# The second layer's modulation in a two-layer diffusion trunk: the context's gate and FFN entries are no longer computed

## The chip, the cores and the metric

The kernel runs on one core of one Trainium2 chip. The metric is the device time of one execution in microseconds (us). The kernel before was timed in three runs: 1600.06, 1601.11 and 1597.38, median 1600.06. All traces are of single profiled executions, and times in them count from the first instruction of the span.

## The reference, cut to what matters

Two streams run through two layers: 512 latent tokens `x` and 256 context tokens `ctx`, each 1024 wide. Each layer makes six modulation vectors of 1024 entries for each stream from one weight matrix `ada_w[layer]` (1024 x 6144): shift, scale and gate of the attention (0, 1, 2), and shift, scale and gate of the FFN (3, 4, 5).

```python
for layer in range(DEPTH):                      # DEPTH = 2
    ctx_out = layer < DEPTH - 1
    mod_x = split(silu(c) @ ada_w[layer] + ada_b[layer], 6)
    mod_c = split(silu(c_ctx) @ ada_w[layer] + ada_b[layer], 6)
    h_x = modulate(rmsnorm(x, norm_g[layer, 0]), mod_x[0], mod_x[1])
    h_c = modulate(rmsnorm(ctx, norm_g[layer, 0]), mod_c[0], mod_c[1])
    o_x, o_c = mixer(...)                       # latents read latents and context
    x = x + mod_x[2] * o_x
    h_x = modulate(rmsnorm(x, norm_g[layer, 1]), mod_x[3], mod_x[4])
    x = x + mod_x[5] * swiglu(h_x, w1[layer], w3[layer], w2[layer])
    if ctx_out:
        ctx = ctx + mod_c[2] * o_c
        h_c = modulate(rmsnorm(ctx, norm_g[layer, 1]), mod_c[3], mod_c[4])
        ctx = ctx + mod_c[5] * swiglu(h_c, w1[layer], w3[layer], w2[layer])
return rmsnorm(x, final_g)
```

In the last layer (`ctx_out` false) the context is only read by the attention: `mod_c[2]` to `mod_c[5]` of that layer appear in nothing that is returned.

## The kernel before, in words

Activations lie transposed: 1024 features as 8 tiles of 128 partitions, tokens along the free side. Every matmul of full precision is done in three, with each operand split into a high and a low half (`hi`, `lo`, both fp32r): hi x hi, hi x lo, lo x hi. The tiles of weights are therefore called `wh` and `wl`. A weight tile is made from a raw load in one of two ways. `split` (L198, L199) copies the high half on ScalarE (ACT) and subtracts on VectorE (DVE). `split_by_dma` (L203 to L205) writes the negative rounded value on ACT (L203), lets a DMA issued by GpSimd (POOL) add the raw value to it (L204), and copies the high half on ACT (L205).

The program runs in stages. The first 460 us hold the first layer's attention, up to 980 us follows the first layer's FFN, to 1232 us the second layer's attention, and then the second FFN and the final norm.

The change is in the first FFN. Its hidden tiles are worked on in pairs p = 0 to 10, grouped as [0, 1], [2], [3, 4], [5, 6], [7, 8], [9, 10] (`supers0`). From pair 2 on, a pair's product with w1 or with w3 is made by `seven` (L1512 to L1551): seven half-size products instead of eight, 84 matmuls of 384 columns, whose sums are formed on DVE out of PSUM (tile `f`). After the w1 product comes the SiLU on ACT (L1620); after the w3 product DVE multiplies (L1627), ACT casts the high half of `g` (L1632) and DVE subtracts the low half (L1632). L1531 copies the first of the seven products out of PSUM on ACT. After a group's first w1 product the group before it goes through its down product with w2 (`down`, L1561 to L1563), whose results are added to the residuals on DVE (L1555). So PE's order is, for instance: pair 5 w1, down of [3, 4], pair 5 w3, pair 6 w1, pair 6 w3, pair 7 w1, down of [5, 6], pair 7 w3.

The weights for `seven` also need sums of quarters of the raw tiles, made on DVE (L534, L535, L538, L539); L538 writes over raw data that the DMA of L204 has to have read. `wh` and `wl` have three buffers each, so a split can begin only when PE is done with the product three steps before, and raw tiles have three buffers too.

The second layer's modulation is computed in the same stretch, on DVE, as rows. `ada1` lists 52 rows: 4 of the first layer, then 8 for each of the six entries of the second layer. For a row, SyncE (SP) loads 128 x 1024 of the transposed `ada_w` (512 KB, two buffers, L623). DVE then multiplies it with the silu of `c` (tile `tables`, L271) and once more with the silu of `c_ctx` (tile `csr`, L272), and an accumulator sums along the row, which gives 128 entries of the vector for each stream. After a vector's eighth row L274 adds the bias, and for the scales L259 forms `amod`. `rows(n, after)` places n rows behind a given instruction: one or two with each step of the down products and one with most products of `seven`. The first 20 rows are the first layer's last four and the second layer's shift and scale of the attention; the other 32 are the entries 2 to 5. After the last row the tiles `tables` and `csr` are used again: L1435 and L1436 load the rope tables into `tables` from POOL's queue.

The order of the first layer's start is written by hand. Behind that (`by_hand.close()`) a planner with its own timeline sets the order of each engine's queue, under the constraints that `tc.issue_after` gives; each queue then runs in that order.

Of the kernel before, what the change touches and what calls it, by code (L numbers as in the profile page):

```python
# [11 lines left out]
ALU = mybir.AluOpType  # L12
# [3 lines left out]
P = 128  # L16
D = 1024
KT = D // P
# [19 lines left out]
def tile_trunk(  # L38
# [27 lines left out]
    nc = tc.nc  # L66
# [35 lines left out]
    adab = const.tile([P, 2, 6, KT], F32, name="adab")  # L102
    ng = const.tile([P, 2, 2, KT], F32, name="ng")
# [5 lines left out]
    mod = [const.tile([P, 6, 2, KT], F32, name=f"mod{l}") for l in range(2)]  # L109
    amod = [const.tile([P, 2, 2, KT], F32, name=f"amod{l}") for l in range(2)]  # L110
# [130 lines left out]
    def ada_out(sb, psum, pieces):  # L241

        pt = psum()
        for hh in range(2):
            nc.tensor.transpose(pt[:, hh * P : (hh + 1) * P], sb[:, hh * P : (hh + 1) * P], ident)
        for hh in range(2):
            src = pt[:, hh * P : (hh + 1) * P].rearrange("p (j w) -> p w j", w=32)[:, 0:2, :]
            for j0, nj, l, s, k0 in pieces:
                dst = mod[l][:, s, :, k0 : k0 + 2 * nj].rearrange("p v (j h) -> p v j h", h=2)[:, :, :, hh]
                b = adab[:, l, s, k0 : k0 + 2 * nj].rearrange("p (j h) -> p h j", h=2)[:, hh : hh + 1, :]  # L250
                nc.vector.tensor_add(dst, src[:, :, j0 : j0 + nj], b.to_broadcast([P, 2, nj]))
        for j0, nj, l, s, k0 in pieces:
            ada_scale(l, s, slice(k0, k0 + 2 * nj))

    def ada_scale(l, s, ks):

        if s in (1, 4):
            nk = ks.stop - ks.start
            nc.vector.scalar_tensor_tensor(  # L259
                amod[l][:, s // 3, :, ks],  # L260
                mod[l][:, s, :, ks],
                1.0,
                ng[:, l, s // 3 : s // 3 + 1, ks].to_broadcast([P, 2, nk]),
                op0=ALU.add,
                op1=ALU.mult,
            )

    def ada_rows(l, s, k, cs, raw, junk):

        col = mod[l][:, s, :, k : k + 1]  # L270
        nc.vector.scalar_tensor_tensor(junk, raw, 1.0, cs[0], op0=ALU.mult, op1=ALU.mult, accum_out=col[:, 0])  # L271
        nc.vector.scalar_tensor_tensor(junk, raw, 1.0, cs[1], op0=ALU.mult, op1=ALU.mult, accum_out=col[:, 1])  # L272
        if k == KT - 1:
            nc.vector.tensor_add(mod[l][:, s], mod[l][:, s], adab[:, l, s : s + 1, :].to_broadcast([P, 2, KT]))  # L274
            ada_scale(l, s, slice(0, KT))


# [349 lines left out]
    with ExitStack() as st:  # L627
# [625 lines left out]
        def row_pieces(n):  # L1253

            def f(s_, k):
                if (s_, k) == (2, 0):
                    load_rows([tables, rbuf])
                junk = rp.tile([P, NX], F32, tag="ru", name="junk", bufs=1).bitcast(mybir.dt.bfloat16)
                raw = S.next()
                if s_ < 5:  # L1260
                    return ada_rows(0, s_, k, [tables, rbuf], raw, junk)

                with tc.issue_after(last_sum[0].ins):
                    ada_rows(0, s_, k, [tables, rbuf], raw, junk)

            out_ = []
            for _ in range(n):
                s_, k = rows.pop(0)
                S.add(ada_wT0[s_ - 2, k] if s_ < 5 else ada_wT[k], "ada")
                out_.append(lambda s_=s_, k=k: f(s_, k))  # L1270
            return out_
# [116 lines left out]
    with ExitStack() as st:  # L1388
# [13 lines left out]
        junk = fp.tile([P, 1024], mybir.dt.bfloat16, name="junk")  # L1402
# [22 lines left out]
        def rows(n, after):  # L1425

            for _ in range(n):
                if ada_raw:
                    with tc.issue_after(after.ins):
                        ada_rows(*ada1[len(ada1) - len(ada1_load) - len(ada_raw)], csr, ada_raw.pop(0), junk)  # L1430
                        ada_request(apool)
# [739 lines left out]
```

## Time and profile before

| what | value |
|---|---|
| timed runs, median of 3 | 1600.06 us |
| profiled execution | 1595.57 us |
| its span | 1593.8 us, granted TensorE clock 0.995 |
| PE busy | 1544.4 us (97%) |
| weight loads on PE (PEld) busy | 1380.3 us (87%) |
| DVE busy | 1246.6 us (78%) |
| ACT busy | 735.4 us (46%) |
| POOL busy | 261.4 us (16%) |
| the first FFN, 459.5 to 980 | PE 516.69 of 520.50 us, DVE 430.73 |
| rows of weights (L271, L272) from 470 on | 52 each, 63.4 us each on DVE |

In a row of a group the profile gives line, engine, operation, tiles out<-in, shape and count, then busy time in us and the mean ns of one, then the idle time before it and what ended that. In a row of the timeline stand the start, the duration, the engine and the line. In a row of waits: who waited, for whom, the us in total, how often, and the longest. PE means matmuls, whose ends are modelled, and PEld their weight loads, which overlap them.

### The profile page before, as it was taken

To read this page: it belongs to the slowest core of one execution; us is meant where nothing else is said; L and a number is where in the kernel's file an instruction comes from. 1 tells how busy PE (TensorE), PEld (TensorE's weight loads), DVE (VectorE), ACT (ScalarE), POOL (GpSimd) and SP (SyncE) were. 2 spreads that over 40 slices of the span, in tenths; PEclk is the share of its full clock that TensorE was granted. 3 is DMA by queue.
4 is the path that set the end of the run, shared out by engine and by line. 5 is a ranking of instruction groups with operands and counts; after the bars stand their busy time and mean duration, and the time that the engine had idled before them with its cause. 6 is when DMAs were issued, how large, how long until landed. Compare 5 with 4: busy or idle time off the path is not lost.

```text
span 1593.8 us, 25582 instructions
## 1 busy us (share of the span) xinstructions
PE 1544.4 (97%) x9902; PEld 1380.3 (87%) x9902; DVE 1246.6 (78%) x2137; ACT 735.4 (46%) x1278; POOL 261.4 (16%) x303
## 2 busy tenths in 40 slices
PE   8999999999999999999999999999999999999997
PEld 5798988877788999989999998886778899989896
DVE  4777798867698789879798867687776887869686
ACT  4546555445354423433324254456764543425354
POOL 1032223462010000000101001254331000000001
PEclk9999999999999999999999999999999999999998
DMA  9322254543236466476757651410002342322321
GB/s 355 110 61 82 77 167 136 180 132 100 69 114 172 109 182 171 133 199 172 216 167 191 179 148 66 118 55 27 28 28 77 109 146 80 130 70 93 119 80 54
DMA packets 68449, 195.28 MB, mean 123 GB/s; under 512 B 6772, under 2 KB 19220, under 8 KB 68328
## 3 DMA queue, kind: packets, MB, share of 16 engines
q1 hardware_dynamic: 58136, 159.95, 31.2%
q0 software_dynamic: 9184, 32.39, 9.5%
q8 instruction: 78, 1.28, 0.3%
q10 hardware_dynamic: 1008, 1.31, 0.2%
q14 instruction: 43, 0.35, 0.1%
HBM read 160.45 MB, written 4.86 MB: 104 GB/s over the span
## 4 chain that ended last, share of the span: by engine, by line
PE 61%; DVE 5%; DMA 2%; issue 1%; ACT 1%; POOL 0%; DVEq 0%; POOLq 0%; ACTq 0%; SPq 0%
PE f L1522 5%; PE f L1520 5%; PE f L1521 5%; PE f L1952 4%; PE f L1951 4%; PE f L1950 4%; PE f L1562 3%; PE f L1561 3%; PE f L1563 3%; PE f L210 3%; PE f L211 3%; PE f L209 3%; PE f L2003 2%; PE f L2004 2%; PE f L2005 2%; PE t L410 2%
## 5 line engine op out<-in xcount | busy, mean ns | idle before, releaser
L198 ACT ACTIVATE wh<-raw 128x1024 fp32r<-128x1024 f32 (+1 forms) x96 | 92.2, 977 | 233.5 <-DVE raw L539 101.5
L209 PE MATMUL lin<-hb,wh 128*128 128x512 f32 (+1 forms) x440 | 157.3, 358 | 4.2 <-ACT hb L1293 1.8
L210 PE MATMUL lin<-hb,wh 128*128 128x512 f32 (+1 forms) x440 | 154.7, 352 | 0.5 <-DVE hb L1294 0.5
L211 PE MATMUL lin<-hb,wl 128*128 128x512 f32 (+1 forms) x440 | 154.2, 350 | 0.0
L199 DVE TENSOR_TENSOR wl<-raw,wh 128x1024 fp32r<-128x1024 f32 (+1 forms) x96 | 107.0, 1120 | 37.1 <-ACT wh L198 35.0
L271 DVE SCALAR_TENSOR_TENSOR junk<-raw,tables 128x1024 bf16<-128x1024 f32 x80 | 98.7, 1234 | 21.0 <-DMA raw<-in_ada_wT_dram 20.5
L204 POOL DMA_DIRECT2D wl<-raw x39 | 34.0, 873 | 443.9 <-ACT wl L203 367.0
L1561 PE MATMUL f<-g,wh 128*128 128x512 f32 (+1 forms) x304 | 102.8, 339 | 0.4 <-DVE s L1550 0.4
L1562 PE MATMUL f<-g,wh 128*128 128x512 f32 (+1 forms) x304 | 102.8, 339 | 0.0
L1951 PE MATMUL f<-hb,wh 128*128 128x256 f32 x360 | 101.7, 283 | 0.0
L1950 PE MATMUL f<-hb,wh 128*128 128x256 f32 x360 | 101.4, 283 | 0.0
L1952 PE MATMUL f<-hb,wl 128*128 128x256 f32 x360 | 101.2, 283 | 0.0
L1563 PE MATMUL f<-g,wl 128*128 128x256 f32 (+1 forms) x304 | 100.6, 336 | 0.0
L209 PEld LDWEIGHTS lin<-hb,wh 128*128 128x128 f32 x440 | 83.2, 189 | 18.6 <-issue 2.7
L1520 PE MATMUL f<-hb,wh 128*128 128x384 f32 x288 | 96.2, 334 | 0.0
L1521 PE MATMUL f<-hb,wh 128*128 128x384 f32 x288 | 96.2, 334 | 0.0
L1522 PE MATMUL f<-hb,wl 128*128 128x384 f32 x288 | 96.2, 334 | 0.0
L210 PEld LDWEIGHTS lin<-hb,wh 128*128 128x128 f32 x440 | 83.4, 189 | 11.0 <-DVE hb L1294 0.7
L211 PEld LDWEIGHTS lin<-hb,wl 128*128 128x128 f32 x440 | 83.3, 189 | 10.5
L161 DVE TENSOR_TENSOR wl<-raw,wh 128x1024 fp32r<-128x1024 f32 x57 | 74.5, 1309 | 15.9 <-ACT wh L160 15.8
L160 ACT CAST wh<-raw 128x1024 fp32r<-128x1024 f32 x57 | 59.7, 1048 | 55.3 <-PE t L210 14.9
L338 POOL TENSOR_TENSOR ns_a<-ns_a,ns_s 128x256 f32<-128x256 f32 (+1 forms) x12 | 12.2, 1019 | 420.7 <-ACT ns_s L334 414.1
(435 smaller groups left out, 4864.0 us busy)
## 6 DMA issues: line engine op xcount, KB each, us to landing
raw<-in_w_dram SPq DMA_DIRECT2D x132, 512.0 KB, 3.8
raw<-in_ada_wT_dram SPq DMA_DIRECT2D x80, 512.0 KB, 4.0
wl<-raw POOLq DMA_DIRECT2D x39, 512.0 KB, 6.6
raw<-in_w_ab_dram SPq DMA_DIRECT2D x24, 512.0 KB, 3.9
raw<-in_ada_w_dram SPq DMA_DIRECT2D x12, 512.0 KB, 8.1
raw<-in_w_c_dram SPq DMA_DIRECT2D x12, 512.0 KB, 3.5
nb<-in_na_bias_dram POOLq DMA_DIRECT2D x16, 256.0 KB, 3.3
raw<-in_wo_ab_dram SPq DMA_DIRECT2D x8, 512.0 KB, 3.5
```

Source lines behind the costliest of these rows:

```text
L209: nc.tensor.matmul(ps, wh(k), xh(k), start=k == 0, stop=False)
L210: nc.tensor.matmul(ps, wh(k), xl(k), start=False, stop=False)
L211: end = nc.tensor.matmul(ps, wl(k), xh(k), start=False, stop=k == n - 1)
L1520: nc.tensor.matmul(ps, wh(k), b[:, 0, :], start=k == 0, stop=False)
L1521: nc.tensor.matmul(ps, wh(k), b[:, 1, :], start=False, stop=False)
L1522: nc.tensor.matmul(ps, wl(k), b[:, 0, :], start=False, stop=k == 3)
L1561: nc.tensor.matmul(ps, hi, g[:, 0, cols[v]], start=first, stop=False)
L1562: nc.tensor.matmul(ps, hi, g[:, 1, cols[v]], start=False, stop=False)
L1563: nc.tensor.matmul(ps, lo, g[:, 0, cols[v]], start=False, stop=last)
L1950: nc.tensor.matmul(ps, wh(k), b[:, 0, :], start=k == 0, stop=False)
L1951: nc.tensor.matmul(ps, wh(k), b[:, 1, :], start=False, stop=False)
L1952: nc.tensor.matmul(ps, wl(k), b[:, 0, :], start=False, stop=k == 3)
```

## The change

`sides(l, s)` says for how many streams an entry of a layer is computed: one, the latent, for the second layer's entries 2 to 5, and two elsewhere. `ada_rows` then issues one accumulating instruction a row and not two, and the bias addition and the `amod` of these entries cover 8 columns and not 16. All rows of weights are still loaded.

```diff
+    def sides(l, s):
+
+        return 1 if l and s > 1 else 2
+
     def ada_scale(l, s, ks):
 
         if s in (1, 4):
-            nk = ks.stop - ks.start
+            nk, nv = ks.stop - ks.start, sides(l, s)
             nc.vector.scalar_tensor_tensor(
-                amod[l][:, s // 3, :, ks],
-                mod[l][:, s, :, ks],
+                amod[l][:, s // 3, 0:nv, ks],
+                mod[l][:, s, 0:nv, ks],
                 1.0,
-                ng[:, l, s // 3 : s // 3 + 1, ks].to_broadcast([P, 2, nk]),
+                ng[:, l, s // 3 : s // 3 + 1, ks].to_broadcast([P, nv, nk]),
                 op0=ALU.add,
                 op1=ALU.mult,
             )
 
     def ada_rows(l, s, k, cs, raw, junk):
 
-        col = mod[l][:, s, :, k : k + 1]
-        nc.vector.scalar_tensor_tensor(junk, raw, 1.0, cs[0], op0=ALU.mult, op1=ALU.mult, accum_out=col[:, 0])
-        nc.vector.scalar_tensor_tensor(junk, raw, 1.0, cs[1], op0=ALU.mult, op1=ALU.mult, accum_out=col[:, 1])
+        col, n = mod[l][:, s, :, k : k + 1], sides(l, s)
+        for i in range(n):
+            nc.vector.scalar_tensor_tensor(junk, raw, 1.0, cs[i], op0=ALU.mult, op1=ALU.mult, accum_out=col[:, i])
         if k == KT - 1:
-            nc.vector.tensor_add(mod[l][:, s], mod[l][:, s], adab[:, l, s : s + 1, :].to_broadcast([P, 2, KT]))
+            nc.vector.tensor_add(mod[l][:, s, 0:n], mod[l][:, s, 0:n], adab[:, l, s : s + 1, :].to_broadcast([P, n, KT]))
             ada_scale(l, s, slice(0, KT))
```

Because a planner sets the order, other instructions move as well, from the down product of [3, 4] to the end of the first FFN; outside it every queue keeps its order. In the changed kernel the lines from 259 on have numbers higher by 4, and L271 and L272 are one line, L276.

The first place is DVE's queue in the down product of [3, 4], before the change. `junk` with `tables` is the latent's sum of a row, `junk` with `csr` the context's, `res` with `f` and `mod` a residual addition, and `raw` with `res` a sum of weight quarters.

```order
L271 SCALAR_TENSOR_TENSOR junk,mod_111<-raw,tables 128x1024
L272 SCALAR_TENSOR_TENSOR junk,mod_111<-raw,csr_4798 128x1024
L1555 SCALAR_TENSOR_TENSOR res<-f,mod_110,res 128x512
L1555 SCALAR_TENSOR_TENSOR res<-f,mod_110,res 128x256
L1555 SCALAR_TENSOR_TENSOR res<-f,mod_110,res 128x512
L1555 SCALAR_TENSOR_TENSOR res<-f,mod_110,res 128x256
L271 SCALAR_TENSOR_TENSOR junk,mod_111<-raw,tables 128x1024
L272 SCALAR_TENSOR_TENSOR junk,mod_111<-raw,csr_4798 128x1024
L271 SCALAR_TENSOR_TENSOR junk,mod_111<-raw,tables 128x1024
L538 TENSOR_TENSOR raw<-res,raw 128x512
L272 SCALAR_TENSOR_TENSOR junk,mod_111<-raw,csr_4798 128x1024
L539 TENSOR_TENSOR raw<-raw 128x512
```

The same place after the change:

```order
L276 SCALAR_TENSOR_TENSOR junk,mod_111<-raw,tables 128x1024
L539 TENSOR_TENSOR raw<-raw 128x512
L199 TENSOR_TENSOR wl<-res,wh 128x512
L1559 SCALAR_TENSOR_TENSOR res<-f,mod_110,res 128x512
L1559 SCALAR_TENSOR_TENSOR res<-f,mod_110,res 128x256
L1559 SCALAR_TENSOR_TENSOR res<-f,mod_110,res 128x512
L1559 SCALAR_TENSOR_TENSOR res<-f,mod_110,res 128x256
L276 SCALAR_TENSOR_TENSOR junk,mod_111<-raw,tables 128x1024 x2
L542 TENSOR_TENSOR raw<-res,raw 128x512
L1559 SCALAR_TENSOR_TENSOR res<-f,mod_110,res 128x512
L1559 SCALAR_TENSOR_TENSOR res<-f,mod_110,res 128x256
L543 TENSOR_TENSOR raw<-raw 128x512
```

The sums with `csr` are gone, a row with `tables` has moved behind the four residual additions, and the sums of quarters (L538, now L542) have fewer rows ahead of them.

The second place is ACT's queue from pair 6's w1 to pair 6's w3, before the change; `wl<-raw` (L203) is the first step of `split_by_dma`, `g<-q` the cast behind a w3 product and `q<-q` the SiLU.

```order
L205 CAST wh<-raw 128x1024
L203 ACTIVATE wl<-raw 128x1024
L1632 CAST g<-q 128x1536
L1531 COPY s<-f 128x384
L198 ACTIVATE wh<-res 128x512
L198 ACTIVATE wh<-raw 128x1024 x2
L205 CAST wh<-raw 128x1024
L203 ACTIVATE wl<-raw 128x1024
L1620 ACTIVATE q<-q 128x1536
L1531 COPY s<-f 128x384
```

After the change:

```order
L205 CAST wh<-raw 128x1024
L1636 CAST g<-q 128x1536
L1535 COPY s<-f 128x384
L203 ACTIVATE wl<-raw 128x1024
L198 ACTIVATE wh<-res 128x512
L198 ACTIVATE wh<-raw 128x1024 x2
L1624 ACTIVATE q<-q 128x1536
L1535 COPY s<-f 128x384
L205 CAST wh<-raw 128x1024
L203 ACTIVATE wl<-raw 128x1024
```

The first L203 has moved behind the cast of g and a copy, the second with its L205 behind the SiLU and a copy. A third L203, ahead of the down product, moves behind a cast and a copy in the same way, and all three moves occur again one group later.

The third place is POOL's queue near the end of the first FFN, before the change; all rows are issues of DMAs, and `tables<-in_rope_dram` are the loads of the rope tables.

```order
L1400 DMA csr_4798<-crow_dram 128x1024
L204 DMA wl<-raw 128x1024 x37
L1435 DMA tables<-in_rope_dram 128x512
L1436 DMA tables<-in_rope_dram 128x512
L204 DMA wl<-raw 128x1024 x2
L204 DMA T<-raw 128x1024 x2
```

After the change:

```order
L1404 DMA csr_4798<-crow_dram 128x1024
L204 DMA wl<-raw 128x1024 x36
L1439 DMA tables<-in_rope_dram 128x512
L1440 DMA tables<-in_rope_dram 128x512
L204 DMA wl<-raw 128x1024 x3
L204 DMA T<-raw 128x1024 x2
```

One DMA that completes a low half has moved behind the two loads of rope tables.

## The prediction

> **What bounds the kernel now.** I read the views in this order: the page's first line, the stage table by windows, the waits of TensorE, then short windows in which TensorE does the same work beside more or less work of VectorE. The span is on the page:
>
> ```profile
> span 1593.8 us, 25582 instructions
> ```
>
> The profiled execution took 1595.57 us in all, so 1.8 us lie outside the span; the median of the three timed runs, 1600.06, is 4.5 us above it. The sums below are differences, and I add them to the median.
>
> The row of the windows view from the first row of weights whose arithmetic the change halves (690.7) to the end of the last one (914), first its column heads:
>
> ```profile
> core 0: us, PE busy (x) PEld busy (x) DVE busy (x) ACT busy (x) POOL busy (x), PEclk, DMA share, GB/s
> 690.70:914.00 223.30, 223.30 (x1286) 211.96 (x1285) 191.80 (x324) 76.77 (x83) 17.70 (x21) 1.00 0.68 187
> ```
>
> PE is busy for all of the stretch at clock 1.00, while DVE is busy for 86% of it. The waits of PE from 470 to 1000, the whole first FFN and a little more:
>
> ```profile
> PE t L209 <- ACT hb L353: 1.5, 1, 1.5
> PE f L1522 <- DVE wl L199: 0.5, 1, 0.5
> PE f L1562 <- DVE g L1632: 0.4, 1, 0.4
> PE f L1561 <- DVE s L1550: 0.4, 1, 0.4
> PE t L210 <- DVE hb L354: 0.2, 1, 0.2
> ```
>
> Five waits, 3.0 us. The PE column above has no hole, so none of them lies between 690.7 and 914: two DVE waits (0.5 and 0.4) come before the changed rows, the rest (2.1) after them. A busy PE row could still hide a slow one. So I compare five stretches in which PE does the same 84 matmuls of 384 columns (one product of `seven` for w1 or w3, with the count a record or two higher from neighbours at the edges):
>
> ```profile
> 637.68:652.25 14.57, 14.57 (x86) 14.57 (x86) 13.37 (x22) 5.67 (x7) 0.87 (x1) 1.00 0.49 128
> 729.54:744.10 14.56, 14.56 (x85) 14.56 (x85) 13.19 (x22) 6.40 (x7) 0.87 (x1) 1.00 0.60 162
> 744.10:758.66 14.56, 14.56 (x85) 14.56 (x85) 14.24 (x25) 6.28 (x7) 0.87 (x1) 1.00 0.61 152
> 913.20:927.76 14.56, 14.56 (x86) 14.56 (x85) 12.40 (x21) 6.51 (x7) 0.90 (x1) 1.00 0.50 136
> 927.76:942.32 14.56, 14.56 (x86) 14.56 (x85) 10.96 (x19) 10.01 (x10) 1.41 (x2) 1.00 0.40 108
> ```
>
> They take 14.56 us whether DVE is busy for 14.24 us of it with modulation rows (744.10) or for 10.96 with none (927.76). That is 14.56/84 = 0.173 us a matmul. TensorE bounds the stage, and DVE's load does not touch its pace as long as DVE keeps up.
>
> **The change part by part.** The removed instructions, from the groups of DVE between 690.7 and 914:
>
> ```profile
> L272 DVE SCALAR_TENSOR_TENSOR junk<-raw,csr 128x1024 bf16<-128x1024 f32 x32 | 39.0, 1220 | 0.3
> ...
> L274 DVE TENSOR_TENSOR mod<-mod,adab 128x16 f32<-128x16 f32 x3 | 0.5, 171 | 0.0
> ```
>
> and one of them with its neighbours in DVE's timeline:
>
> ```profile
> 745.06 1.22 DVE L272 SCALAR_TENSOR_TENSOR junk<-raw,csr 128x1024 bf16<-128x1024 f32 x1
> 746.20 0.08 DVE L272 DVE_READ_ACCUMULATOR junk<-raw,csr 128x1 f32 x1
> 746.20 0.55 DVE L1537 TENSOR_TENSOR s<-f,s 128x384 f32<-128x384 f32 x1
> ```
>
> The accumulating instruction holds DVE from 745.06 to 746.20, and the read of its accumulator overlaps the next one. So 32 x 1.14 = 36.5 us of DVE's queue go. The four bias additions (L274, one of them just outside this window) and the one scale (L259) go from 16 to 8 columns: between nothing and all of 5 x 0.17 = 0.9 us of DVE; I take nothing, because they are small enough to be all overhead. On the path that sets the end the 37 us are worth 0.0 us, because PE covers them: it never waits in that stretch. Were the cover gone, all of it could show, 36.5 us.
>
> Nothing is added, and all 32 rows of weights (512 KB each) are still loaded, since the latent's sum reads them.
>
> What moves is the order around it. DVE's queue comes to the same work earlier: the order shows that the residual additions (L1555) and L538 stand behind fewer sums. Sooner on DVE means weight buffers free sooner, so loads start sooner; this costs nothing by itself. ScalarE's queue is the place where something is put later. In the two groups of pairs that end in the down products at 773.22 and 865.05, `split_by_dma` has its first step (L203) behind the cast of g (L1632) or the SiLU (L1620) and behind the copy L1531, at three places each. Behind L203 stand POOL's DMA (L204), and then PE, which needs the low half of the weights that this DMA writes.
>
> The first place: L203 of pair 6's w3 weights, and the same step one group earlier (pair 4's w3), where the kernel before already has the order L1632, L1531, L203:
>
> ```profile
> 735.25 1.05 ACT L203 ACTIVATE wl<-raw 128x1024 fp32r<-128x1024 f32 x1
> ```
>
> ```profile
> 642.87 1.48 ACT L1632 CAST g<-q 128x1536 fp32r<-128x1536 f32 x1
> 644.24 0.48 ACT L1531 COPY s<-f 128x384 f32<-128x384 f32 x1
> 644.61 1.07 ACT L203 ACTIVATE wl<-raw 128x1024 fp32r<-128x1024 f32 x1
> ```
>
> POOL's issues of three of these DMAs, and the time to landing of four (from the DMA view, one window for each issue: at 645.97, 736.60, 658.74 and 765.20):
>
> ```profile
> 736.60 0.87 POOL L204 DMA_DIRECT2D wl<-raw  x1 [14.21 <-ACT wl L203]
> 751.67 0.87 POOL L204 DMA_DIRECT2D wl<-raw  x1 [14.20 <-ACT wl L203]
> 765.20 0.88 POOL L204 DMA_DIRECT2D wl<-raw  x1 [12.66 <-ACT wl L203]
> ```
>
> ```profile
> wl<-raw POOLq DMA_DIRECT2D x1, 512.0 KB, 4.6
> wl<-raw POOLq DMA_DIRECT2D x1, 512.0 KB, 7.1
> wl<-raw POOLq DMA_DIRECT2D x1, 512.0 KB, 8.4
> wl<-raw POOLq DMA_DIRECT2D x1, 512.0 KB, 6.4
> ```
>
> Counted from the start of PE's product, L203 stands at 735.25 - 729.54 = 5.71 us now, and at 644.61 - 637.68 = 6.93 where it is behind the other two. So I expect it 1.22 later: the issue at 737.82. PE's first use of the low half is the third matmul from 744.10, 744.45. With 4.6 us to landing (the group that had the order already) it is there at 742.4; with 7.1 at 744.9, a wait of 0.5; with 8.4 at 746.2, a wait of 1.8. I take no wait, because the 4.6 belongs to the same order, and with DVE ahead the loads that ran beside it in the other case come earlier.
>
> The second place is pair 7's w1, behind the SiLU and L1531. Pair 5's w1 had that order already with the DMA that took 8.4, and none of PE's waits lies there: 0.0.
>
> The third place has no such forerunner: the first w2 piece of the down product at 773.22.
>
> ```profile
> 763.85 1.05 ACT L203 ACTIVATE wl<-raw 128x1024 fp32r<-128x1024 f32 x1
> 765.36 1.48 ACT L1632 CAST g<-q 128x1536 fp32r<-128x1536 f32 x1 [0.45 <-DVE q L1627]
> 766.74 0.47 ACT L1531 COPY s<-f 128x384 f32<-128x384 f32 x1
> ```
>
> ```profile
> 773.69 0.40 PE L1563 MATMUL f<-g,wl 128*128 128x512 f32 x1
> ```
>
> L203 behind these two starts at 766.74 + 0.37 = 767.11 (0.37 as from 644.24 to 644.61), 3.26 later, and the DMA is issued at 768.46. With 4.6 to landing: 773.1, no wait. With its own 6.4: 774.9, a wait of 1.2 (against 773.69). With 8.4: 3.2. One or two removed sums ahead of the cast (1.14 each) may bring it forward. I take 0.3, nearest to the 4.6 row, and the ends 0 and 3.2.
>
> The sum: 2 groups x (0 + 0 + 0.3) = +0.6 us. Upper end 2 x (1.8 + 3.2) = +10; lower end -0.4, if the wait of L1562 on g (0.4), at 953, went too; I leave it, because the chain of waits leads from it back to loads of weights, not to the removed sums.
>
> The Trainium skill's page "DMA: Bandwidth & Descriptors" (Anatomy of one DMA, SWDGE path) fits a DMA issued from GpSimd with 2.0 us plus bytes over 436 GB/s: an estimate by that page is 3.2 us for 512 KB, and the sum by it would be 0.0. The rows above (4.6 to 8.4, for a DMA that also accumulates) disagree, and they decide.
>
> POOL's queue has one move: an L204 goes behind the two loads of rope tables, which wait for the last reader of `tables`.
>
> ```profile
> 905.17 0.87 POOL L204 DMA_DIRECT2D wl<-raw  x1 [20.04 <-ACT wl L203]
> 911.27 0.57 POOL L1435 DMA_DIRECT2D tables<-in_rope_dram  x1 [5.23 <-DVE junk L271]
> ```
>
> If that reader stayed at its place, L204 would issue 7 us late; PE needs it at 913.20 + 0.35, and with the 7.1 from above it lands at 912.3 as it is. But the eight sums of the last down product (9.1 us) are gone ahead of that reader, so I expect it before 905: 0.0, with the 7 at the far end. On SyncE's queue w and modulation loads change places by one; each then starts when its buffer is free, and I take 0.
>
> **The rivals.** *The late split, slower.* At the first and third place the DMA takes 7.1 and 6.4 as now, so PE waits 0.5 + 1.2 in each of two groups: +3.4, 1603.5. It decides by the landing against 744.45 and 773.69 on the old clock. For it: these durations stood at just these places. Against it: the earlier group. Chance 0.14.
>
> *DVE sets the pace, faster.* If the PE row hid time, the weight loads would show it: 223.30 - 211.96 = 11.3 us without one, so -11.3, 1588.8. Against it: in the five equal stretches loads fill 14.56 of 14.56 whatever DVE does, so the rest lies in the down products with their longer matmuls. Chance 0.06. The Trainium skill's "Perfetto Trace Analysis" (Identifying the Most-Contended Engine) says that matmul busy time is a poor measure and that the share of weight loads is to be read; by that rule this rival has its 5%, and the stretches do not bear it out.
>
> That the change does not do what it says is excluded: 32 sums fewer stand in DVE's order.
>
> **How the numbers follow.** Likeliest: 1600.06 + 0.6 = 1600.7, chance 0.80. Timed runs of one kernel lay between 1597.38 and 1601.11; I take 0.2% (3.2 us) for what a measurement can tell from no change. A median of three may be off by 1.5 (the three spread over 3.7). The range reaches below by that and by the 2.7 of the lowest run under its median (1596.5), and above to the slower rival plus 1.5 (1605.0). Faster 0.06, same 0.80, slower 0.14.
>
> **What would show it.** Right: 32 fewer L272-like sums, DVE about 39 to 42 us less busy, the products still at 14.56, no PE wait on L204's landing over 0.5. Wrong: products longer than 14.6 around 744, 773, 836 or 865, or shorter than 14.5 (DVE did matter), or an L204 at 905 that waits for L271.

## The result, and the profile after

The changed kernel is slower. Over 20 timed runs each, the median went from 1599.75 us to 1606.18 us; the ratio is 1.0040, with a 95% interval from 1.0031 to 1.0050, so between 5.0 and 8.0 us were lost. The forecast was 1600.7, no measurable difference, with a range up to 1605.0.

The profiled execution of the changed kernel took 1609.54 us, 3.4 above its median; that of the kernel before was 4.2 below its own. So the two traces lie 14 us apart where the medians lie 6.4 apart, and a difference between two spans is not the size of the effect. I look for the waits that one trace has and the other lacks.

The waits of PE from 470 to 1000 in the changed kernel (lines 4 higher than before):

```profile
PE f L1526 <- DMA wl<-raw: 4.7, 1, 4.7
PE t L209 <- ACT hb L357: 1.5, 1, 1.5
PE f L1567 <- DMA wl<-raw: 1.4, 2, 1.1
PE f L1526 <- DVE wl L199: 1.1, 1, 1.1
PE f L1565 <- DVE s L1554: 0.6, 1, 0.6
PE t L210 <- DVE hb L358: 0.2, 1, 0.2
```

Two of the rows are new, and both are waits for L204, the DMA that completes a low half: one of 4.7 us in a product of `seven`, and two of 1.4 together in down products. (The wait of 1.1 for L199 lies at 601, ahead of the changed rows; it was 0.5 before.) The windows view shows the products (columns as in the prediction); the three rows are pair 6's w1, pair 6's w3 and pair 10's w1, with edges up to 0.2 us beside those of the products:

```profile
733.40:747.96 14.56, 14.56 (x86) 14.56 (x85) 12.90 (x21) 6.41 (x7) 0.87 (x1) 1.00 0.59 165
747.96:762.52 14.56, 14.56 (x86) 14.56 (x85) 10.80 (x18) 6.29 (x7) 0.87 (x1) 1.00 0.54 149
919.21:941.60 22.39, 17.71 (x86) 17.39 (x86) 14.62 (x23) 7.46 (x9) 0.89 (x1) 0.85 0.47 116
```

The products still take 14.56 us, now with VectorE busy for 10.80 to 12.90 of them, where it was busy for 14.24 in one before. Only pair 10's w1 product, from 919.22 to 941.43, takes 22.2: 7.7 us more for the same matmuls. GpSimd's timeline says why (start, duration, engine, line; in brackets the idle time and what ended it):

```profile
916.59 0.57 POOL L1439 DMA_DIRECT2D tables<-in_rope_dram  x1 [25.43 <-DVE junk L276]
917.15 0.57 POOL L1440 DMA_DIRECT2D tables<-in_rope_dram  x1
917.71 0.94 POOL L204 DMA_DIRECT2D wl<-raw  x1
```

```profile
909.85 1.05 ACT L203 ACTIVATE wl<-raw 128x1024 fp32r<-128x1024 f32 x1
```

L203 was done at 910.9, but its DMA was issued at 917.71. It stood behind the two loads of rope tables, and these waited until 916.59 for a sum (`junk`, L276) to be done with their buffer. The chain of waits, in order of time (start, duration, what), ends with just these:

```profile
913.93 1.22 DVE wl L199
915.15 1.15 DVE junk L276 x2
916.30 0.29 issue
916.59 0.50 POOL tables L1439
...
917.15 0.56 POOL tables L1440
917.71 6.84 DMA wl<-raw
```

The 6.84 at the end is the DMA itself, landed at 924.55, where PE had come to it at 919.57 + 0.17 = 919.7 (the start of the matmul ahead, and the pace of 0.173).

Where the removed work on VectorE went is in its groups. First two rows of the kernel before between 690.7 and 914, then the same two lines after, between 690.7 and 918 (busy time, mean, then the idle time before them and what ended it):

```profile
L534 DVE TENSOR_TENSOR res<-raw 128x512 f32<-128x512 f32 x10 | 6.9, 690 | 14.0 <-DMA raw<-in_w_dram 14.0
...
L538 DVE TENSOR_TENSOR raw<-res,raw 128x512 f32<-128x512 f32 x10 | 6.9, 686 | 2.2 <-DMA wl<-raw 2.1
```

```profile
L538 DVE TENSOR_TENSOR res<-raw 128x512 f32<-128x512 f32 x10 | 6.9, 693 | 27.0 <-DMA raw<-in_w_dram 27.0
...
L542 DVE TENSOR_TENSOR raw<-res,raw 128x512 f32<-128x512 f32 x9 | 6.2, 691 | 19.1 <-DMA wl<-raw 19.1
```

VectorE waits 27.0 - 14.0 = 13.0 us longer for loads of weights and 19.1 - 2.2 = 16.9 longer for the accumulating DMA: 29.9 of the 36.5 us that were removed are now waiting for transfers. Most of the rest is a longer wait for PE's down products (L1555, now L1559): 14.6 us and not 6.8.

### The profile page after: what moved, and what is told of

It is laid out like the page before. It is cut to its first block, busy times and chain, and to the rows that moved or that the text cites. A ratio compares the mean times of both kernels' runs of the same rounds, so it can differ in the third digit from the quotient of the medians.

```text
span 1607.8 us, 25509 instructions
## 1 busy us (share of the span) xinstructions
PE 1551.9 (97%) x9902; PEld 1386.0 (86%) x9902; DVE 1211.6 (75%) x2073; ACT 736.9 (46%) x1278; POOL 261.6 (16%) x303
## 4 chain that ended last, share of the span: by engine, by line
PE 46%; DVE 7%; DMA 6%; issue 6%; ACT 2%; POOL 1%; DVEq 0%; POOLq 0%; ACTq 0%; SPq 0%
DMA wl<-raw 5%; PE f L1956 4%; PE f L1955 4%; PE f L1954 4%; PE f L1567 2%; PE f L1565 2%; PE f L1566 2%; PE f L2008 2%; PE f L2009 2%; PE f L2007 2%; PE f L1526 2%; PE f L1525 2%; PE t L414 2%; PE f L1524 2%; PE t L1761 2%
## 5 line engine op out<-in xcount | busy, mean ns | idle before, releaser
L209 PE MATMUL lin<-hb,wh 128*128 128x512 f32 (+1 forms) x440 | 157.3, 358 | 5.1 <-ACT hb L1297 2.4
L210 PE MATMUL lin<-hb,wh 128*128 128x512 f32 (+1 forms) x440 | 155.1, 352 | 0.4 <-DVE hb L1298 0.4
L199 DVE TENSOR_TENSOR wl<-raw,wh 128x1024 fp32r<-128x1024 f32 (+1 forms) x96 | 107.0, 1123 | 39.5 <-ACT wh L198 37.4
L276 DVE SCALAR_TENSOR_TENSOR junk<-raw,tables 128x1024 bf16<-128x1024 f32 x80 | 99.0, 1238 | 14.9 <-DMA raw<-in_ada_wT_dram 14.6
L204 POOL DMA_DIRECT2D wl<-raw x39 | 34.2, 876 | 433.2 <-ACT wl L203 399.7
L209 PEld LDWEIGHTS lin<-hb,wh 128*128 128x128 f32 x440 | 83.3, 189 | 19.6 <-ACT hb L1297 2.9
L210 PEld LDWEIGHTS lin<-hb,wh 128*128 128x128 f32 x440 | 83.5, 190 | 11.0 <-DVE hb L1298 0.6
```

Of the source, the lines that this page charges most:

```text
L209: nc.tensor.matmul(ps, wh(k), xh(k), start=k == 0, stop=False)
L210: nc.tensor.matmul(ps, wh(k), xl(k), start=False, stop=False)
```

## The experiments

All times are medians. Each ratio compares a kernel with runs of the kernel before on the same chip, so a ratio tells more than the difference of two medians; the changed kernel's is 1.0040. The intervals reach 0.13 to 0.28% (2 to 4.5 us) to each side. Theory A: the DMA behind the rope loads is most of the loss, the late split at the third place the rest. Theory B: the late split is most of it. Theory C: something spread out. The first, second and third place are, as in the prediction, the three moves of L203 on ScalarE. Line numbers shift by a few between the kernels: L210 and L209 are what L204 and L203 are here. In the diffs `negated` and `added` list the instructions of L203 and L204 as they are made, and `queue_behind(a, b)` gives the planner the order b, a without a wait.

**The rope loads behind the DMA again.**

```diff
-        nc.gpsimd.dma_start(f32(lo), src, accum_op=ALU.add)
+        added.append(nc.gpsimd.dma_start(f32(lo), src, accum_op=ALU.add))
...
-            nc.gpsimd.dma_start(cost, rope[1, 0])
-            nc.gpsimd.dma_start(sint, rope[1, 1])
+            with tc.issue_after(added[36].ins):
+                nc.gpsimd.dma_start(cost, rope[1, 0])
+                nc.gpsimd.dma_start(sint, rope[1, 1])
```

> The changed kernel, with the two loads of rope tables queued on GpSimd behind the DMA that completes the low half of pair 10's w1 weights, as in the kernel before. Theory A (that DMA's place behind the rope loads, which wait for the last sum that reads their buffer, is most of the loss): PE's wait of 4.7 us on wl near 918 us is gone, and with it the slower matmuls behind it; 5 to 8 us less than the changed kernel, 1599 to 1602. Theory B (the late split at the three places of ScalarE's queue is most of it): no difference, 1605 to 1607, and no wait at 918 either way. Theory C (something spread over the first FFN, such as loads that collide elsewhere): at most 2 us less, and waits of PE at other places.

Measured: 1601.36, ratio 1.0005 (0.9990 to 1.0021). GpSimd's timeline, and the one row of PE's waits for a DMA from 690 to 930:

```profile
906.98 0.87 POOL L210 DMA_DIRECT2D wl<-raw  x1 [20.04 <-ACT wl L209]
911.21 0.57 POOL L1446 DMA_DIRECT2D tables<-in_rope_dram  x1 [3.35 <-DVE junk L282]
```

```profile
PE f L1574 <- DMA wl<-raw: 1.8, 2, 1.0
```

The DMA is issued at 906.98, before the rope loads, and the long wait is gone; the waits left (1.8) are those of the third place. Most of the loss came back, as theory A has it.

**The rope loads first, in the kernel before.** The opposite edit: the DMA is made to queue behind the second rope load, with all sums kept.

```diff
-            nc.gpsimd.dma_start(sint, rope[1, 1])
+            queue_behind(added[36], nc.gpsimd.dma_start(sint, rope[1, 1]))
```

> The kernel before, all its sums kept, with only the two loads of rope tables queued ahead of that same DMA; the planner moves some matmuls of the product around it by a few places. Theory A: the sum that reads the tables last runs at 909.7, so the rope loads are issued at 911.3 and 911.8 and the DMA at 912.4 and not at 905.2; with 7 us to landing it is there at 919.4, and PE, which needs it at 913.6, waits about 5 us: 3 to 7 us more than the kernel before, 1603 to 1607. Theories B and C: no difference, 1599 to 1601.

Measured: 1604.78, ratio 1.0029 (1.0010 to 1.0048).

```profile
918.60 0.57 POOL L1441 DMA_DIRECT2D tables<-in_rope_dram  x1 [27.42 <-DVE junk L277]
...
919.71 0.94 POOL L210 DMA_DIRECT2D wl<-raw  x1
```

```profile
PE f L1528 <- DMA wl<-raw: 2.7, 1, 2.7
```

The order on one queue alone, with nothing removed, makes the kernel slower, by 1.6 to 7.7 us. The wait is shorter than forecast (2.7 and not 5): in PE's timeline the planner has put six high-half matmuls at the head of the product, where the order was two high, one low, and the wait comes some 2.6 us into the product and not at its third matmul.

**L203 first at the third place**, in the changed kernel. The cast of g is traced a little later, in the product behind it, and queued behind the L203 of the first w2 piece.

```diff
+                    def cast(g=g, q=q, last=last):
+                        with tc.issue_after(negated[last].ins) if last else nullcontext():
+                            hi = nc.scalar.copy(g[:, 0, :], q)
```

> The changed kernel, with L203 put ahead of the cast of g and of the copy again at the third place of both groups (the first w2 piece of the down products of [5, 6] and [7, 8]); the loads of rope tables stay ahead of the DMA. Theory A: the two waits of PE on wl in the down products (1.1 and 0.3 us in the profile, 1.8 us with their edges) go and the one of 4.7 us stays: 1 to 2 us less than the changed kernel, 1604 to 1605. Theory B: most of the loss goes, 1600 to 1602. Theory C: no difference, 1606.

Measured: 1602.98, ratio 1.0021 (1.0007 to 1.0035). The waits in the down products are gone; of PE's waits on L204 only that of the rope loads is left, at 914, and it is 2.3 in this trace:

```profile
PE f L1532 <- DMA wl<-raw: 2.3, 1, 2.3
```

The gain is 0.19%, 3.0 us, more than the 1 to 2 expected, though the intervals would allow those, and less than theory B needs.

**Both** (called below the kernel with both places mended).

> The changed kernel with both of these: the rope loads behind the DMA, and L203 first at the third place of both groups. Theory A together with the late split as the small rest: the removed sums themselves are worth nothing, so the time is that of the kernel before, within 0.2%: 1597 to 1602. If the 32 sums were worth something on the path, it would be faster than before by more than 0.2%. Theory C: still 1603 to 1606.

Measured: 1597.93, ratio 0.9989 (0.9976 to 1.0002). The four kernels add up: the rope order is worth 0.40 - 0.05 = 0.35% by the first experiment and 0.21 + 0.11 = 0.32% between the last two, the third place 0.40 - 0.21 = 0.19% and 0.05 + 0.11 = 0.16%. That is 5.1 to 5.6 us and 2.6 to 3.0 us. Taken with its two intervals, each of these differences is uncertain by 0.17 to 0.20%, about 3 us: the rope order is clear of that, the third place hardly, though its waits are seen to go in the traces. What is left, the change itself with 36 us less on VectorE, is not to be told from no change.

**The last reader sooner.** POOL's order stays as in the changed kernel; only the rows move.

```diff
-                        down(hidden(supers0[n - 1]), (1,) if n == 2 else (2,))
+                        down(hidden(supers0[n - 1]), (1,) if n == 2 else (3,) if n == 5 else (2,))
```

> The changed kernel, with the last six rows placed three behind each of the first two steps of the last down product, and not two behind each of the first three. GpSimd's queue stays as in the changed kernel, with the rope loads ahead of the DMA of pair 10's w1; only the last reader of their buffer, on VectorE, comes one step (about 12 us) sooner. Theory A (the wait of the rope loads for that reader, not their own 1.1 us on the queue, is the loss): the rope loads are issued about 907, the DMA at 911 as soon as its L203 is done, and lands before PE needs it; 5 to 8 us less than the changed kernel, 1599 to 1602. Theory D (the rope loads cost the DMA by their place alone, by issue time and by the transfers that they put beside it): the wait near 918 stays over 2 us, 1604 to 1606.

The expectation miscounts the rows: the last eight stood two behind each of four steps, and stand now three, three and two behind the first three. The last reader is one step sooner, as it says. Measured: 1599.14, ratio 1.0000 (0.9987 to 1.0012).

```profile
903.24 0.57 POOL L1439 DMA_DIRECT2D tables<-in_rope_dram  x1 [15.03 <-DVE mod L278]
...
908.26 0.90 POOL L204 DMA_DIRECT2D wl<-raw  x1 [3.89 <-ACT wl L203]
```

The rope loads stand ahead of the DMA and cost nothing that can be measured: their own wait is over at 903.24, and the DMA then waits 3.89 us more for its L203. It is the wait at the head of the queue that costs, not the place (theory D falls).

**VectorE with less again** (the vectors of the 32 rows are not made).

```diff
+            w = slice(0, 64 if n == 1 else 1024)
-            nc.vector.scalar_tensor_tensor(junk, raw, 1.0, cs[i], op0=ALU.mult, op1=ALU.mult, accum_out=col[:, i])
+            nc.vector.scalar_tensor_tensor(junk[:, w], raw[:, w], 1.0, cs[i][:, w], op0=ALU.mult, op1=ALU.mult, accum_out=col[:, i])
```

> The kernel with both places mended (rope loads behind the DMA, L203 first at the third place), and in addition the latent's 32 sums of the second layer's entries 2 to 5 cover only 64 of 1024 columns, so that those vectors are not made; their rows are loaded as before. VectorE does some 33 us less again. Theory A (VectorE is covered by PE in this stretch): no difference from the kernel with both places mended, within 0.2%, 1595 to 1601. If VectorE's queue still held something up: faster by over 3 us, below 1595.

Measured: 1607.77, ratio 1.0046 (1.0029 to 1.0062): slower than the kernel before, which neither branch has. PE's waits between 690 and 914:

```profile
PE f L1534 <- DMA wl<-raw: 7.6, 3, 3.8
```

Two lie at the first place, in pair 6's w3 at 745 and pair 8's w3 at 844 (3.0 and 3.8); the third, 0.9, is in pair 8's w1 at 829. One can follow the first back. Two rows of the windows view, 722.1 to 727.1 of the kernel with both places mended and of this one:

```profile
722.10:727.10 5.00, 5.00 (x31) 5.00 (x30) 5.00 (x10) 0.37 (x1) 0.87 (x1) 1.00 0.75 139
```

```profile
722.10:727.10 5.00, 5.00 (x31) 5.00 (x30) 4.52 (x10) 0.70 (x2) 0.87 (x1) 1.00 0.86 196
```

VectorE is through sooner, loads of rows and of weights start sooner, and more is moved (196 against 139 GB/s) beside the L204 issued at 722: it takes 7.3 us and not 5.1. VectorE waits for it, then casts and products come later, and L203 behind the cast of g is at 739.77 and not 738.05:

```profile
729.74 0.69 DVE L549 TENSOR_TENSOR raw<-res,raw 128x512 f32<-128x512 f32 x1 [3.01 <-DMA wl<-raw]
...
738.02 1.48 ACT L1649 CAST g<-q 128x1536 fp32r<-128x1536 f32 x1 [2.26 <-DVE q L1640]
...
739.77 1.07 ACT L209 ACTIVATE wl<-raw 128x1024 fp32r<-128x1024 f32 x1
```

Its DMA in turn takes 7.4 and not 4.7. So the slack of the first place was small. In this trace the longer times of the two DMAs used it up; that a VectorE with less to do is what lengthened them is argued from the order of these rows, not tested by itself.

**L203 ahead of the SiLU too** (the second place), whole sums, both places mended; the SiLU is traced later, in the same way as the cast.

> The kernel with both places mended, and in addition L203 put ahead of the SiLU at the second place, for the w1 weights of pairs 5, 7 and 9. The profile of the kernel with both places mended has waits of PE on wl there of 0.5 and 0.8 us. Theory A: these go, 0.5 to 1.5 us less than with both places mended, 1596 to 1598, which would be faster than the kernel before by 0.15% or more. If the DMA's time to landing and not its start is what is late: no difference, 1598 to 1599.

Measured: 1598.01, ratio 0.9989 (0.9976 to 1.0002); a wait of 0.7 on wl stays. No difference.

**Sums doubled, in the kernel before.**

```diff
+        if l and s > 1:
+            nc.vector.scalar_tensor_tensor(junk, raw, 1.0, cs[1], op0=ALU.mult, op1=ALU.mult, accum_out=col[:, 1])
```

> The kernel before, with the context's sum of each of the 32 rows computed twice: 32 x 1.14 = 36.5 us more on VectorE between 690 and 914, where it was busy for 191.8 of 223.3 us. Theory A (PE covers VectorE, with 31 us to spare): the cover is used up, VectorE becomes the bound of this stretch, PE waits there, and the time is 5 to 20 us above the kernel before, 1605 to 1620. If VectorE's sums were free to spread beyond the stretch: no difference, 1599 to 1602.

Measured: 1614.40, ratio 1.0083 (1.0055 to 1.0111). PE's two longest waits between 690 and 914:

```profile
PE f L1563 <- ACT g L1634: 6.2, 1, 6.2
PE f L1565 <- DMA wl<-raw: 2.3, 1, 2.3
```

The size fits theory A, the way does not. VectorE was busy for 195.5 of the 224 us from 690 to 914, hardly more than in the kernel before (192.5), so it did not become the bound of the stretch; PE's waits for VectorE's own results come to 3.0 us there. PE's longest wait is for a cast of g on ScalarE, which stood in ScalarE's queue behind a split that waited 9.02 us for a load of weights. That load was issued at 872.08, when L199 on VectorE was done with its buffer (872.06), and landed after 11.35 us. So in this wait the extra sums reached PE by way of a late buffer, a long load and another engine's queue, and not by a result of VectorE that PE reads. How much of the 14 us went this way stays open.

**Rows not loaded**, both places mended: the last 32 sums read a row that is there already.

```diff
+            raw = held_raw[0] if len(ada1_load) <= 32 else pool.tile([P, 1024], F32, tag="ada", name="raw")
...
+            if raw is not held_raw[0]:
+                nc.sync.dma_start(raw, ada_wT[KT // 2 + n])
```

> The kernel with both places mended, in which the last 32 rows of weights (the second layer's entries 2 to 5) are not loaded: their sums read the row loaded last, so these vectors are wrong and only the time counts. The queues of TensorE, ScalarE and GpSimd are the same. Theory E (the loads of rows beside the accumulating DMAs make these take 6 to 8 us and not 4.6, and that is what PE's waits on wl come from): the DMAs of L204 between 690 and 914 land 4.5 to 5.5 us after their issue, no wait of PE on wl is over 0.2 us there, and the time is 1 to 3 us below that of both places mended, 1595 to 1597. If the time to landing belongs to those DMAs themselves: they take as long as before and the time is the same, 1597 to 1599.

Measured: 1597.77, ratio 0.9989 (0.9973 to 1.0005). The DMAs of L204 between 690 and 914 (count, KB, median us to landing), first of the kernel with both places mended, then of this one:

```profile
wl<-raw POOLq DMA_DIRECT2D x19, 512.0 KB, 6.2
```

```profile
wl<-raw POOLq DMA_DIRECT2D x20, 512.0 KB, 5.2
```

The loads of rows make the DMA longer by 1.0 us in the median: theory E is right on that. It is wrong on the time: PE still waits 0.9 us once (0.8 with both places mended), and nothing that can be measured is gained. What else makes these DMAs last longer at one time than at another was not tested.

**The first place too, with sums of 64 columns** (the vectors are not made): the cast of g behind L203 also for pairs 6 and 8.

> The kernel with the sums of 64 columns (the vectors of entries 2 to 5 are not made), in which L203 is put ahead of the cast of g at the first place too, for the w3 weights of pairs 6 and 8. Theory F (the 9 us that this kernel lost came from the split behind the cast of g at the first place, where PE waited 3.1 and 3.8 us with slower matmuls behind them): the two waits go, and the time falls by 7 to 10 us to that of both places mended, 1597 to 1600. If an idle VectorE lets loads collide whatever the order on ScalarE: less than half of it comes back, 1603 to 1608.

Measured: 1602.50, ratio 1.0014 (0.9997 to 1.0031).

```profile
PE f L1575 <- DMA wl<-raw: 0.7, 1, 0.7
```

The 7.6 us of waits at 745, 829 and 844 are gone from the trace; the wait left is in a down product. In time 0.32% came back, 5 us of the 9: more than half, less than theory F has, with an uncertainty of 0.24% or 4 us that would still allow it. What the rest is, stays open.

**All three places first**, whole sums, rope loads behind the DMA.

> The changed kernel with every L203 of the first, second and third places ahead of the cast of g or the SiLU, as in the kernel before or sooner, and the rope loads behind the DMA. All sums of the latent are whole. Theory A: what is left is the change alone. If the removed sums are worth nothing on the path: the same as both places mended, 1597 to 1599, within 0.2% of the kernel before. If the change is worth something once the order is right: below 1596.8, that is over 0.2% faster than the kernel before.

Measured: 1601.26, ratio 1.0002 (0.9984 to 1.0020). With everything put back, the change is worth nothing that can be measured. No version was found that beats the kernel before; the best is 0.9989, with an interval that holds 1.

## Why the prediction was wrong, point by point

**The bound, right.** PE bounds the stage and VectorE does not set its pace. With both places mended, 32 sums fewer give 0.9989; the products stay at 14.56 us.

**The removed sums at 0.0, right.** The 36.5 us of VectorE were covered. They went into its own waits for transfers (29.9 us by the two groups above).

**The first place at 0.0, right.** L203 runs at 740.92, 740.92 - 733.54 = 7.4 us behind the start of the product (6.93 were expected), since the cast before it waits for VectorE; its DMA lands after 4.8, and PE does not wait. For this kernel the range's 1.8 was enough. The margin was thin all the same: in the kernel with sums of 64 columns PE waited 3.0 and 3.8 us there.

**The third place, mechanism right, size too small.** The sum had 0.3 for each group, 0.6 in all; the trace has waits of 1.1 and 0.3, and the runs give 2.6 to 3.0 us. ScalarE's timeline:

```profile
769.79 1.49 ACT L1636 CAST g<-q 128x1536 fp32r<-128x1536 f32 x1 [1.85 <-DVE q L1631]
771.18 0.47 ACT L1535 COPY s<-f 128x384 f32<-128x384 f32 x1
771.54 1.06 ACT L203 ACTIVATE wl<-raw 128x1024 fp32r<-128x1024 f32 x1
```

The product began at 762.66, so L203 is 8.9 behind it; forecast were 767.11 - 758.66 = 8.45. The larger part is the DMA, 6.0 to landing where I had taken 4.6 as the nearest row. Its own 6.4 was the better guess: a row from the same place, with the same transfers around it, is nearer than one that only shares the order.

**The POOL move at 0.0, wrong, and this is the step that failed.** It said: "But the eight sums of the last down product (9.1 us) are gone ahead of that reader, so I expect it before 905: 0.0, with the 7 at the far end." The pair 10 w1 product starts at 913.20 before and at 919.22 after. Counted back from that, the last reader starts 3.5 us ahead of it before (909.74) and 4.2 after (915.06): it came 0.7 sooner, not five. The prediction's own sign of being wrong, "an L204 at 905 that waits for L271", is what happened.

The step treats VectorE's queue as if only work filled it: take sums out, and what stands behind them comes sooner by as much. VectorE's timeline shows where it had to wait on the way to the reader, first before, then after the change:

```profile
888.63 1.22 DVE L271 SCALAR_TENSOR_TENSOR junk<-raw,tables 128x1024 bf16<-128x1024 f32 x1 [0.72 <-DMA raw<-in_ada_wT_dram]
...
891.18 0.69 DVE L538 TENSOR_TENSOR raw<-res,raw 128x512 f32<-128x512 f32 x1 [1.31 <-DMA wl<-raw]
```

```profile
892.24 1.23 DVE L276 SCALAR_TENSOR_TENSOR junk<-raw,tables 128x1024 bf16<-128x1024 f32 x1 [1.90 <-DMA raw<-in_ada_wT_dram]
...
899.84 0.69 DVE L542 TENSOR_TENSOR raw<-res,raw 128x512 f32<-128x512 f32 x1 [6.37 <-DMA wl<-raw]
...
906.57 1.14 DVE L1559 SCALAR_TENSOR_TENSOR res<-f,mod,res 128x512 f32<-128x512 f32 x2
910.52 0.69 DVE L538 TENSOR_TENSOR res<-raw 128x512 f32<-128x512 f32 x1 [2.81 <-DMA raw<-in_w_dram]
911.13 1.14 DVE L1559 SCALAR_TENSOR_TENSOR res<-f,mod,res 128x512 f32<-128x512 f32 x2
...
915.06 1.22 DVE L276 SCALAR_TENSOR_TENSOR junk<-raw,tables 128x1024 bf16<-128x1024 f32 x1
```

Before, these waits are 2.0 us; after, 11.1. So 9.1 us of sums were counted as gone (seven of the eight, 8.0 us, stood ahead of the reader; the eighth, at 912.83, stood behind it), and 9.1 us of waits for transfers came in their place. Two transfers set the reader's time. L542 waits for an L204 issued 28.9 us ahead of the product in both kernels (884.26 and 890.29); it landed after 6.7 us before and after 9.4 now. Behind L542 stands the split L199 (904.29), which frees the buffer for the next load of weights; that load was issued at 905.54 and took 5.0 us, where it took 3.6 before. L538 waits for it, and behind L538 stand the last residual additions and the reader. PE is not what holds the additions: their down product ended by 904.65, and they ran at 906.57 and 911.13.

A second trace bears this out. In the changed kernel with L203 first at the third place, VectorE has the same order here, but that L204 took 5.9 us, the wait in front of the same sum of quarters was 2.03 and not 6.37, the reader came 6.6 us ahead of the product (907.21 and 913.76), and PE waited 2.3 us and not 4.7. Why that DMA lasts 9.4 us at one time and 5.9 at another is not shown.

Part of it could have been read from the trace before. L538 at 891.18 already waits there for L204, so the sums ahead of it cannot bring the reader forward; only the four between it and the reader can, 4.6 us, which puts the reader's start at 905.2 and not before. The rope loads were issued 1.5 behind that start and cost 1.1, so by this estimate the DMA starts at 907.8 and, with 7.1 to landing, is there at 914.9, where PE needs it at 913.55: a wait of 1.3. On that clock the reader started at 909.0, 3.8 us later still, about as much as the two transfers took longer (2.7 and 1.4).

The 7 us were meant for the DMA's start; the wait that came of it in the trace was 4.7, and slow matmuls behind it made 7.7 for the product. Over all runs the rope order cost 5.1 to 5.6 us.

**The rivals.** The late split was there, and its 3.4 us are near the 2.6 to 3.0 measured, but partly by luck: it had given the third place 2.4 and the first place 1.0, and the first place cost nothing. VectorE does not set the pace. The rope order had an end of 7 in the working but no case of its own, and so no part in the range, which ended 1.5 above the late split. It was the larger of the two.

## What to carry to other kernels

Work that is taken off a covered engine is worth nothing by itself, but it changes what a planner puts where, and a wait at the head of an in-order queue holds all that stands behind it: of every instruction that moved behind another one, ask what that other one waits for, and whether that wait can end sooner at all. Work taken out of a queue brings what stands behind it forward only as far as no transfer is waited for on the way: here 9.1 us of sums became 9.1 us of waiting. And an engine with less to do is not always harmless to the engine that bounds: with 33 us less again on VectorE the kernel lost 0.57%, 9 us, and two of the DMAs on the way to PE's wait took 7.3 and 7.4 us in the trace where they had taken 5.1 and 4.7.

## What the runs showed of the hardware

**A wait of PE can cost more than its length.** Rows of the windows view of the changed kernel, from the end of the 4.7 us wait on (PEclk is the third column from the end):

```profile
924.00:927.00 3.00, 2.41 (x8) 2.41 (x9) 2.40 (x5) 0.90 (x1) 0.00 (x0) 0.50 0.00 0
927.00:930.00 3.00, 3.00 (x11) 3.00 (x11) 3.00 (x6) 1.11 (x2) 0.00 (x0) 0.50 0.05 4
```

For 6 us the granted clock is 0.50, and 11 matmuls run in 3 us where 3/0.173 = 17 would; such slow matmuls are about 3 of the 7.7 us lost. After the wait of 2.7 us (rope loads first, kernel before) the clock was 0.51 from 924.8 to 928; after that of 2.3 us (L203 first at the third place) it stayed at 1.00. The Trainium skill, page "TensorE: Matmul & The Clock Gate", Part 1, says that the clock halves after an idle window of about 3.4 us that runs free of the kernel. The halving agrees with these rows; the length does so only in part, since a wait of 2.7 us already had it. Each of these is one trace.

**The accumulating DMA of 512 KB has no fixed price.** It landed 4.6 to 8.4 us after its issue in the four rows of the prediction and 9.4 after it in the one at 890.29 of the changed kernel, and its median fell from 6.2 to 5.2 when the loads of rows beside it were left out.
